# Scale and shift of four feature chunks by multiply-adds on VectorE instead of float32 products on TensorE

## The chip, the cores and the metric

The kernel runs on one core of a Trainium2 chip. The metric is the device time of one execution in microseconds; the figure compared is the median of several runs. The engines of the core are TensorE (PE; its weight loads are PEld), VectorE (DVE), ScalarE (ACT), GpSimd (POOL) and SyncE (SP, which here only issues transfers). Each executes its own instructions in the order in which the program gives them, and waits on semaphores for the others.

## What is computed

Two layers of an encoder trunk on one sequence of 512 rows and 1024 features, all float32. Each of the four sub-layers begins with an adaLN: the rows are normalised, scaled by `norm_g * (1 + scale)` and moved by `shift`; scale and shift come from a vector `c` through a matrix product. The first sub-layer's mixer is a gated convolution.

```python
mod = (jax.nn.silu(c) @ ada_w + ada_b).reshape(bsz, DEPTH, 2, 3, D_MODEL)
for i in range(DEPTH):
    shift, scale, gate = (mod[:, i, 0, k][:, None, :] for k in range(3))
    h = rmsnorm(x, norm_g[i, 0]) * (1.0 + scale) + shift
    if i % N_MIXERS == 0:
        y = short_conv_mixer(h, a_w_in[j], a_conv_w[j], a_w_out[j])
    ...
    x = x + gate * rmsnorm(y, norm_g[i, 1])
    ...
def short_conv_mixer(h, w_in, conv_w, w_out):
    b_gate, c_gate, v = jnp.split(h @ w_in, 3, axis=-1)
    u = causal_depthwise_conv(c_gate * v, conv_w)
    return (b_gate * u) @ w_out
```

## The kernel before

Matrix products take their float32 operands as two parts, a high part (rounded) and a low part (the rest): three matmuls for each product of a weight tile and an activation tile. Features lie on the 128 partitions in eight chunks, 0 to 7; the 512 rows are the free dimension.

The opening, up to about 60 us, does the first adaLN and the first third of the mixer's input product at once. Its order is written out by hand in the string `OPENING`; every name in it is one step, and the engines get their instructions in that order. Of chunk j, `A` multiplies the vector `csil` (silu of c) with the columns of `ada_w` for the chunk's shift and scale on TensorE (16 small float32 matmuls, line 195), `E` copies the sums out (ScalarE, line 199), `T` transposes them (two matmuls, line 202), and `R` adds the bias and makes `mods` (shift) and `acol` (scale) in three small VectorE operations (lines 205 to 208). `u` makes the chunk's scaled value on VectorE (line 360), `H` its high part on ScalarE (line 362), `l` its low part on VectorE (line 364). A step k`j`_`i` is three matmuls of chunk j with one of six weight tiles into accumulator i (line 975, tiles `li`). The weights come in pairs of chunks: a step w`c`l`j` or w`c`b`j` casts the high part of tiles 0 to 3 or of tiles 4 and 5 (ScalarE, line 845), w`s`l`j` and w`s`b`j` make the low part (VectorE, line 847).

The loads are issued by SyncE in program order. `stage_cols` loads the columns of `ada_w` for one or two chunks (tiles `ada_st`, 512 KB each, line 177), `lead_load` the weights of two chunks (`wst_l`, line 830). At most eight transfers of the queue are under way: each issue waits for the one eight before it to land. Chunks 3 and 4 come in one set of four tiles (two for the shift, two for the scale, split along the 1024 inputs), 5 and 6 in another.

Later sets of `ada_w` are not multiplied on TensorE: `ada_madd` (lines 126 and 128) multiplies and adds 1024 columns at a time on VectorE into `ada_acc`, one operation for each of eight blocks of inputs, `ada_fold` (line 141) sums groups of 32 partitions, and a matmul with the 0/1 matrix `four` (line 148) sums the rest.

After the opening the kernel goes on with the mixer's other products (lines 305 to 307), whose weights come in 1 MB loads (line 222).

Of the kernel before, what the change touches and what calls it, by code (L numbers as in the profile page):

```python
# [31 lines left out]
MUL, ADD, SUB = ALU.mult, ALU.add, ALU.subtract  # L32
# [6 lines left out]
def trunk_kernel(  # L39
# [48 lines left out]
    adab = cols2[:, 0:96]  # L88
# [27 lines left out]
    mods = consts.tile([P, 96], F32, name="mods")  # L116
    acol = consts.tile([P, 32], F32, name="acol")
# [6 lines left out]
    def ada_madd(acc, w, k):  # L124
        if k == 0:
            dve.tensor_scalar(acc, w, csil[:, 0:1], None, MUL)
        else:
            dve.scalar_tensor_tensor(acc, w, csil[:, k:k + 1], acc, MUL, ADD)  # L128
# [9 lines left out]
    def ada_fold(acc, dst):  # L138


        dve.tensor_reduce(dst, acc.rearrange("p (b r) -> p b r", r=32), axis=AX.X, op=ADD, apply_transpose=True)
# [20 lines left out]
    def ncol(s, post, j, n=1):  # L162
        i, sub = divmod(s, 2)
        o = (i * 4 + sub * 2 + post) * 8 + j
        return norm_c[:, o:o + n]

    def ada_stage(j0, n, stage):


        res = []  # L170
        for b in range(2):
            c0 = b * D + j0 * P
            parts = []
            for q in range(n):
                st = stage()
                rows = slice(q * D // n, (q + 1) * D // n)
                dma(st, ada_w[rows, c0:c0 + n * P].rearrange("(k p) f -> p k f", p=P))
                parts.append(st)
            res.append(parts)
        return res  # L180
# [150 lines left out]
    def small(n):  # L331
        return tmp.tile([P, n], F32, tag=f"ss{n}", name="ss", bufs=8)
# [19 lines left out]
    def make_h(s, j, hj, src, sl):  # L352

        n = sl.stop - sl.start
        q = s * 24 + j
        us = []

        def value():
            us.append(t2("u")[:, :n])
            dve.tensor_scalar(us[0], src, acol[:, s * 8 + j:s * 8 + j + 1], mods[:, q:q + 1], MUL, ADD)  # L360

        return (value, lambda: act.activation(hj[:, 0, sl], src, AF.Identity, bias=mods[:, q:q + 1],
                                       scale=acol[:, s * 8 + j:s * 8 + j + 1]),
                lambda: dve.tensor_tensor(hj[:, 1, sl], us[0], hj[:, 0, sl].bitcast(F32), SUB))
# [4 lines left out]
    OPENING = """  # L369
xo0 xo1 xo2 xo3 A0b xo4 E0 xo6 xo5 T0 wcl0 R0 u0 q7 H0 wsl0 wcb0 k0a0 l0 xo7 k0a1 k0a2 k0a3 wsb0  # L370
k0c0 k0_4 A1 k0_5 E1 wcl1 T1 k0c1 wcb1 R1 k0c2 k0c3 k0b0 u1 k0b1 H1 k0b2 wsl1 k0b3 l1 A2 wsb1 k1_0
E2 T2 k1_1 R2 wcl2 k1_2 u2 H2 k1_3 wsl2 k1_4 wcb2 l2 k1_5 wsb2 k2_0 k2_1 k2_2 A3 A4 E3 T3 E4 k2_3 R3
T4 u3 H3 k2_4 R4 k2_5 wcl4 l3 u4 H4 k3_0 wsl4 k3_1 wcb4 k3_2 l4 k3_3 wsb4 k3_4 k3_5 k4_0 A5 A6 E5 T5
E6 k4_1 R5 wcl6 T6 u5 k4_2 H5 R6 k4_3 u6 H6 k4_4 l5 wcb6 A7 l6 wsl6 k4_5 E7 T7 wsb6 k5_0 R7 k5_1 u7
k5_2 H7 k5_3 l7 k5_4 k5_5 k6_0 k6_1 k6_2 k6_3 k6_4 k6_5 k7_0 k7_1 k7_2 k7_3 k7_4 k7_5
"""


# [412 lines left out]
    with ExitStack() as ph:  # L791
        sums_p, first_p = ExitStack(), ExitStack()
        gx = ph.enter_context(tc.tile_pool(name="gx", bufs=1, side="right", reuse_waits="tile"))
        ada_p.append(sums_p.enter_context(tc.tile_pool(name="adap", bufs=3, side="right", reuse_waits="tile")))
        actp = first_p.enter_context(tc.tile_pool(name="actp", bufs=22, reuse_waits="tile"))
        four = gx.tile([P, P], F32, tag="four", name="four", bufs=1)
        ada_acc = ada_p[0].tile([P, D], F32, tag="acc", name="ada_acc", bufs=1)
# [71 lines left out]
        staged = []

        def stage_cols(j0, n):
            cols = ada_stage(j0, n, lambda: actp.tile([P, 8 // n, n * P], F32, tag="a", name="ada_st0"))
            staged.extend([(q, cols) for q in range(n)])
# [4 lines left out]
        def turn(t, j):  # L878
            pe.transpose(xtr[j][:, t * P:(t + 1) * P], xn[t][:, j * P:(j + 1) * P], ident)

        def turned_out(j):
            if j % 2 == 0:
                dve.tensor_copy(xf[j], xtr[j])
            else:
                act.copy(xf[j], xtr[j])

        def busy(dst, n):

            for _ in range(n):
                pe.matmul(dst, ident, ident, start=True, stop=True)  # L890
# [11 lines left out]
        with tc.manual_schedule(engines={PE_ENGINE, mybir.EngineType.SP, mybir.EngineType.Activation,  # L902
# [3 lines left out]
                dma(xt[t], x[0, t * P:(t + 1) * P, :])  # L906
            dma_s(rows[:64, 1, :], norm_g.rearrange("i k (r p) -> (i k r) p", p=P))
            dma_s(rows[:96, 2, :], ada_b.rearrange("(r p) -> r p", p=P))
            stage_cols(0, 1)
            load = lead_load(0, 1)  # L910
            next(load)
            next(load)
            stage_cols(1, 1)
            next(load)
            stage_cols(2, 1)
            list(lead_load(1))
            stage_cols(3, 2)
# [60 lines left out]
            def step(name):  # L978
                kind, i = name[:1], name[1:]
                if name[:2] == "xo":  # L980
                    turned_out(int(name[2:]))
                elif name == "q7":
                    xtr.append(aux_ps("xtr"))
                    for t in range(4):
                        turn(t, 7)
                    busy(acc_of(2)[:, :P], 5)
                    h.extend([hp.tile([P, 2, T], F32R, tag=f"h{j}", name=f"h{j}") for j in range(4, KD)])
                elif kind == "A":
                    j = int(i[0])
                    if j:  # L990
                        mods_[j] = ada_first(j, *staged[j], cpad)
                    next(mods_[j])
                    if j == 0:
                        busy(acc_of(2)[:, :P], 2)
                    if j == 4:
                        list(lead_load(3))
                        stage_cols(7, 1)
                elif kind in "ETR":
                    next(mods_[int(i)])
                elif kind in "uHl":  # L1000
                    j = int(i)
                    if j not in hdo:
                        hdo[j] = make_h(0, j, h[j], xf[j], FULL)
                    hdo[j]["uHl".index(kind)]()
                elif kind == "w":
                    kk = int(name[3:])
                    if kk // 2 not in lead:
                        lead_tiles(kk // 2)
                    lead_split(kk // 2, slice(kk % 2, kk % 2 + 1) if kk < 2 else slice(0, 2),
                               "lb".index(name[2]), "cs".index(name[1]))  # L1010
                    if name == "wsb1":
                        list(lead_load(2))
                        stage_cols(5, 2)
# [44 lines left out]
            splits, ws, acts, us, ggs = [], [], [], {}, []  # L1058
# [142 lines left out]
            for k in range(18):  # L1201
                i, jp = k % 6, 2 + k // 6 * 2
# [305 lines left out]
        with tc.manual_schedule(engines={PE_ENGINE, mybir.EngineType.SP, mybir.EngineType.Activation,  # L1508
# [53 lines left out]
            for u in range(UN1):  # L1562
                v = u - 1
# [98 lines left out]
            for k in range(k0, last + 1):  # L1662
# [10 lines left out]
                q, j = divmod(k - 3, 4)  # L1673
# [105 lines left out]
        h, lead_ps, rest, _ = begun  # L1779

    with ExitStack() as ph:
# [301 lines left out]
        four = uh[:, 0:P]  # L2083
# [405 lines left out]
    with ExitStack() as ph:  # L2489
# [137 lines left out]
        with tc.manual_schedule(engines={PE_ENGINE, mybir.EngineType.SP, mybir.EngineType.Activation,  # L2627
# [60 lines left out]
            for u in range(UN):  # L2688
                v = u - 1
# [98 lines left out]
            st = [{"s2": small(2), "s1": small(1), "b1": small(1)} for _ in range(4)]  # L2788
# [133 lines left out]
```

## Time and profile before

| | |
|---|---|
| median of 3 runs | 1308.82 us (1307.88 to 1308.95) |
| span of the profiled execution | 1307.2 us |
| instructions | 20568 |
| moved by transfers | 241.69 MB, mean 185 GB/s |
| 20 to 40 us: transfers | 339 and 348 GB/s |

All times of the prediction are microseconds from the start of the profiled execution's span; its own total lies 1.6 us under the median. A row of a timeline has start, duration, engine, line, operation, the tile written and the tiles read, the shape, and the count of merged instructions; brackets hold the idle time before it and what ended that. A matmul's recorded duration is longer than its share of the engine, since matmuls are pipelined: the distance between starts counts.

### The profile page before, as it was taken

Reading aid. Unit: us, or ns where it says so; the run is one execution under the profiler, and the core shown is the slowest. Engines: PE = TensorE matmul, PEld = TensorE weight load, DVE = VectorE, ACT = ScalarE, POOL = GpSimd, SP = SyncE. Lnnn points to the kernel's source line nnn. Section 1 sums busy time; section 2 is a strip of 40 time slices with the busy share of each in tenths; the row PEclk is TensorE's granted clock in tenths of the full one; section 3 lists DMA queues with packets and bytes.
Section 4 is the critical chain, followed back from the end, with each engine's and each line's share of the span. In section 5 each row is a group of like instructions: output and inputs, shape, how many; then the busy total and the mean of one; then the engine's idle time right before and its main releaser. Section 6 shows DMA issues by size and latency. Waiting matters only on the chain.

```text
span 1307.2 us, 20568 instructions
## 1 busy us (share of the span) xinstructions
PE 1295.7 (99%) x7841; PEld 1140.6 (87%) x7841; DVE 1045.4 (80%) x1598; ACT 736.0 (56%) x1302; POOL 127.5 (10%) x156
## 2 busy tenths in 40 slices
PE   8999999999999999999999999999999999999998
PEld 7788889999988888898888888888899999998886
DVE  5587998978866986769899998987877777767888
ACT  5423466455532565656765567755764555544665
POOL 0000011111100230000000000000100121101320
PEclk9999999999999999999999999999999999999999
DMA  9779661799868984437664456614432788878961
GB/s 310 229 257 297 185 193 50 204 239 240 202 190 264 261 158 119 144 118 231 219 216 160 141 177 217 185 50 161 145 98 72 190 221 204 205 194 286 176 123 64
DMA packets 225942, 241.69 MB, mean 185 GB/s; under 512 B 10532, under 2 KB 177588, under 8 KB 224820
## 3 DMA queue, kind: packets, MB, share of 16 engines
q1 hardware_dynamic: 203200, 192.87, 47.3%
q0 software_dynamic: 18496, 35.92, 15.1%
q10 hardware_dynamic: 4148, 11.59, 2.7%
q8 instruction: 61, 1.00, 0.3%
q14 instruction: 37, 0.30, 0.1%
HBM read 203.76 MB, written 4.34 MB: 159 GB/s over the span
## 4 chain that ended last, share of the span: by engine, by line
PE 94%; DMA 2%; SPq 2%; DVE 1%; ACT 1%; issue 0%; DVEq 0%
PE sA L693 12%; PE ip L305 11%; PE ip L307 11%; PE ip L306 11%; PE y L408 7%; PE sC L693 6%; PE cA L2624 5%; PE sB L693 3%; PE cA L1483 3%; PE li L305 2%; PE li L307 2%; PE li L306 2%; PE li L975 2%; PE y L1156 1%; PE y L2199 1%; PE yd L2027 1%
## 5 line engine op out<-in xcount | busy, mean ns | idle before, releaser
L305 PE MATMUL ip<-h,whl 128*128 128x512 f32 x640 | 253.0, 395 | 0.2 <-DVE cv L1075 0.2
L307 PE MATMUL ip<-h,whl 128*128 128x512 f32 x640 | 249.7, 390 | 0.0
L306 PE MATMUL ip<-h,whl 128*128 128x512 f32 x640 | 249.6, 390 | 0.0
L305 PEld LDWEIGHTS ip<-h,whl 128*128 128x128 f32 x640 | 120.3, 188 | 25.8 <-issue 1.8
L307 PEld LDWEIGHTS ip<-h,whl 128*128 128x128 f32 x640 | 120.3, 188 | 25.3
L306 PEld LDWEIGHTS ip<-h,whl 128*128 128x128 f32 x640 | 120.4, 188 | 23.8
L693 PE MATMUL sA<-tq,whl 128*128 128x256 f32 x1008 | 130.6, 284 | 0.0
L693 PEld LDWEIGHTS sA<-tq,whl 128*128 128x128 f32 x1008 | 125.5, 192 | 0.3
L232 DVE TENSOR_TENSOR whl<-wst,whl 128x1024 fp32r<-128x1024 f32 x70 | 85.2, 1220 | 23.4 <-ACT whl L231 22.3
L128 DVE SCALAR_TENSOR_TENSOR ada_acc<-ada_st,csil,ada_acc 128x1024 f32<-128x1024 f32 x70 | 89.7, 1282 | 3.2 <-DMA ada_st<-in_ada_w_dram 1.9
L305 PE MATMUL li<-h,whl 128*128 128x256 f32 x288 | 83.7, 290 | 0.0
L307 PE MATMUL li<-h,whl 128*128 128x256 f32 x288 | 81.7, 284 | 0.0
L306 PE MATMUL li<-h,whl 128*128 128x256 f32 x288 | 81.6, 283 | 0.0
L231 ACT CAST whl<-wst 128x1024 fp32r<-128x1024 f32 x70 | 72.6, 1040 | 7.8 <-DMA wst<-in_a_w_in_dram 4.0
L408 PE MATMUL y<-whlo,ys 128*128 128x512 f32 x288 | 67.3, 392 | 0.0
L1870 DVE SCALAR_TENSOR_TENSOR cu<-ip,cols,cu 128x511 f32<-128x511 f32 (+2 forms) x84 | 62.8, 747 | 3.4 <-ACT cu L1867 1.4
L408 PEld LDWEIGHTS y<-whlo,ys 128*128 128x128 f32 x288 | 53.8, 188 | 11.4 <-issue 0.5
L2624 PE MATMUL cA<-whlo,ao 128*128 128x512 f32 x264 | 61.0, 391 | 0.4 <-DVE c L2830 0.2
L2624 PEld LDWEIGHTS cA<-whlo,ao 128*128 128x128 f32 x264 | 49.4, 188 | 11.5 <-ACT whlo L2589 1.2
L305 PEld LDWEIGHTS li<-h,whl 128*128 128x128 f32 x288 | 55.3, 192 | 0.8 <-issue 0.8
L306 PEld LDWEIGHTS li<-h,whl 128*128 128x128 f32 x288 | 55.3, 192 | 0.0
L307 PEld LDWEIGHTS li<-h,whl 128*128 128x128 f32 x288 | 55.2, 192 | 0.0
(457 smaller groups left out, 2740.8 us busy)
## 6 DMA issues: line engine op xcount, KB each, us to landing
ada_st<-in_ada_w_dram SPq DMA_DIRECT2D x96, 512.0 KB, 6.4
wsu<-in_f_w_in_dram SPq DMA_DIRECT2D x30, 512.0 KB, 5.5
sg<-in_f_w_in_dram SPq DMA_DIRECT2D x56, 256.0 KB, 3.4
wsu<-in_f_w_in_dram SPq DMA_DIRECT2D x56, 256.0 KB, 4.7
wst<-in_m_w_in_dram SPq DMA_DIRECT2D x14, 1024.0 KB, 5.9
wst<-in_f_w_in_dram SPq DMA_DIRECT2D x10, 1024.0 KB, 5.1
wst<-in_m_w_in_dram SPq DMA_DIRECT2D x20, 512.0 KB, 5.2
wst<-in_a_w_in_dram SPq DMA_DIRECT2D x9, 1024.0 KB, 6.8
```

Of the source, the lines that this page charges most:

```text
L128: dve.scalar_tensor_tensor(acc, w, csil[:, k:k + 1], acc, MUL, ADD)
L231: later.append((lambda sw=sw, w=w: act.copy(w[:, 0, :nk, :], sw), lambda sw=sw, w=w: dve.tensor_tensor(w[:, 1, :nk, :], sw, w[:, 0, :nk, : ...
L232: lambda sw=sw, w=w: dve.tensor_tensor(w[:, 1, :nk, :], sw, w[:, 0, :nk, :].bitcast(F32), SUB)))
L305: pe.matmul(dst, w_at(w, 0, kk), a[:, 0, sl], start=start, stop=False)
L306: pe.matmul(dst, w_at(w, 0, kk), a[:, 1, sl], start=False, stop=False)
L307: pe.matmul(dst, w_at(w, 1, kk), a[:, 0, sl], start=False, stop=stop)
L408: pe.matmul(pst, a[:, al, tk], wt[:, wl, kk, :], start=i == 0 and k == (opens[hf][t] if opens else 0), stop=k == K - 1 and i == 2, skip_gr ...
L693: pe.matmul(dst, w[:, wl, k0 + k, :], self.moving(q, k, al), skip_group_check=True, start=q in self.FIRST and k == 0 and i == 0, stop=k == ...
L975: pe.matmul(acc_of(i), w[:, part // 2, k, c0:c0 + P], h[kk][:, part % 2, :], start=(kk, part) == (0, 0), stop=(kk, part) == (KD - 1, 2))
L1483: pe.matmul(bank[r, sub], a[:, al, q, tk], w[:, wl, q, :], start=first and k == 0, stop=False, skip_group_check=True)
L1870: dve.scalar_tensor_tensor(u[:, sft:], pst[:, :T - sft], w[3 - sft], u[:, sft:], MUL, ADD)
L2624: pe.matmul(bank[r][sub], a[:, al, q, tk], w[:, hl, q, :], start=first and k == 0, stop=last and k == 2, skip_group_check=True)
```

## The change

Shift and scale of chunks 3 and 4, and of 5 and 6, are now made like the later sets. `stage_two` loads, for two chunks, four tiles each with two blocks of inputs, shift and scale side by side: 512 columns in one row, in two loads of 256 KB. Step `M` is one multiply-add of one block (VectorE, 512 columns), `F` the fold, `P` one matmul with `four`, `G` four adds of the bias and one scale. Chunks 0, 1, 2 and 7 stay with TensorE's products. The value `u` of chunks 3 to 7 is made by ScalarE. The order string has new steps and places; `stage_cols(7)` and the weights of chunks 6 and 7 are issued at another step, at the same place of SyncE's order.

```diff
         def value():
             us.append(t2("u")[:, :n])
-            dve.tensor_scalar(us[0], src, acol[:, s * 8 + j:s * 8 + j + 1], mods[:, q:q + 1], MUL, ADD)
+            if j < 3:
+                dve.tensor_scalar(us[0], src, acol[:, s * 8 + j:s * 8 + j + 1], mods[:, q:q + 1], MUL, ADD)
+            else:
+                act.activation(us[0], src, AF.Identity, bias=mods[:, q:q + 1], scale=acol[:, s * 8 + j:s * 8 + j + 1])
...
-E2 T2 k1_1 R2 wcl2 k1_2 u2 H2 k1_3 wsl2 k1_4 wcb2 l2 k1_5 wsb2 k2_0 k2_1 k2_2 A3 A4 E3 T3 E4 k2_3 R3
-T4 u3 H3 k2_4 R4 k2_5 wcl4 l3 u4 H4 k3_0 wsl4 k3_1 wcb4 k3_2 l4 k3_3 wsb4 k3_4 k3_5 k4_0 A5 A6 E5 T5
-E6 k4_1 R5 wcl6 T6 u5 k4_2 H5 R6 k4_3 u6 H6 k4_4 l5 wcb6 A7 l6 wsl6 k4_5 E7 T7 wsb6 k5_0 R7 k5_1 u7
-k5_2 H7 k5_3 l7 k5_4 k5_5 k6_0 k6_1 k6_2 k6_3 k6_4 k6_5 k7_0 k7_1 k7_2 k7_3 k7_4 k7_5
+E2 T2 k1_1 R2 wcl2 k1_2 u2 H2 k1_3 wsl2 k1_4 wcb2 M3_0 l2 k1_5 M3_1 wsb2 M3_2 M3_3 k2_0 M3_4 M3_5 k2_1
+M3_6 M3_7 F3 k2_2 k2_3 P3 G3 u3 H3 k2_4 u4 H4 k2_5 wcl4 l3 wsl4 k3_0 k3_1 l4 wcb4 k3_2 M5_0 M5_1 wsb4
+k3_3 M5_2 M5_3 k3_4 M5_4 M5_5 k3_5 wcl6 k4_0 M5_6 M5_7 F5 k4_1 k4_2 A7 P5 G5 E7 u5 T7 H5 k4_3 R7 u6 H6
+wcb6 k4_4 l5 wsl6 k4_5 l6 u7 H7 wsb6 k5_0 k5_1 k5_2 l7 k5_3 k5_4 k5_5 k6_0 k6_1 k6_2 k6_3 k6_4 k6_5 k7_0
+k7_1 k7_2 k7_3 k7_4 k7_5
...
+        def stage_two(j0):
+
+            two_st[j0] = [actp.tile([P, 2, 2, 2 * P], F32, tag="a", name="ada_st2") for _ in range(KD // 2)]
+            for q, st in enumerate(two_st[j0]):
+                for b in range(2):
+                    dma(st[:, :, b, :], ada_w[2 * q * P:2 * (q + 1) * P, b * D + j0 * P:b * D + (j0 + 2) * P]
+                        .rearrange("(k p) f -> p k f", p=P))
+
+        def two_madd(j0, k):
+            ada_madd(ada_acc[:, 512:], two_st[j0][k // 2][:, k % 2].rearrange("p b f -> p (b f)"), k)
+
+        def two_fold(j0):
+            part = gx.tile([P, 32], F32, tag="fold", name="fold", bufs=2)
+            two_part[j0] = part[:, :16]
+            ada_fold(ada_acc[:, 512:], two_part[j0])
+
+        def two_sum(j0):
+            pt = aux_ps("ada_p2")
+            pe.matmul(pt[:, :16], four, two_part[j0], start=True, stop=True)
+            two_part[j0] = pt
+
+        def two_mods(j0):
+            m2, b2 = [v[:, 0:16].rearrange("p (a b) -> p a b", b=8)[:, :, j0:j0 + 2] for v in (mods, adab)]
+            src = two_part[j0][:, :16].rearrange("p (a q b) -> p a q b", a=2, b=4)
+            for b in range(4):
+                r = slice(b * 32, (b + 1) * 32)
+                dve.tensor_tensor(m2[r], src[r, :, :, b], b2[r], ADD)
+            dve.scalar_tensor_tensor(acol[:, j0:j0 + 2], mods[:, 8 + j0:10 + j0], 1.0, ncol(0, 0, j0, 2), ADD, MUL)
...
+                elif kind == "M":
+                    two_madd(int(i[0]), int(i[2]))
+                elif kind in "FPG":
+                    (two_fold, two_sum, two_mods)["FPG".index(kind)](int(i))
```

TensorE, from the products of chunk 4 (chunk 3's stand just before them) to chunk 3's lead products, before; the tiles `h_124` and `h_125` are chunks 2 and 3:

```order
L195 MATMUL ada_pe<-ada_st_169,rows 32x128 x4
L195 MATMUL ada_pe<-ada_st_171,rows 32x128 x4
L195 MATMUL ada_pe<-ada_st_173,rows 32x128 x4
L195 MATMUL ada_pe<-ada_st_175,rows 32x128 x4
L202 MATMUL ada_pe<-ident,ada_acc 128x128 x2
L975 MATMUL li<-h_124,whl_l 128x512 x3
L202 MATMUL ada_pe<-ident,ada_acc 128x128 x2
L975 MATMUL li<-h_124,whl_b 128x512 x6
L975 MATMUL li<-h_125,whl_l 128x512 x12
```

The same stretch after the change, from chunk 1's last lead products on (line 975 has become 1009):

```order
L1009 MATMUL li<-h_123,whl_b 128x512 x6
L1009 MATMUL li<-h_124,whl_l 128x512 x12
L898 MATMUL ada_p_472<-fold,four 128x16
L1009 MATMUL li<-h_124,whl_b 128x512 x6
L1009 MATMUL li<-h_125,whl_l 128x512 x12
```

The products and both pairs of transposes are gone; one matmul that reads the fold (P3) stands between the fourth and the fifth of chunk 2's six tiles. The second set has the like: P5 stands behind chunk 7's products, with chunk 4's last nine matmuls behind it.

VectorE, before, from the low part of chunk 2's first weights (`whl_l`) to chunk 3's low part:

```order
L847 TENSOR_TENSOR whl_l<-wst_l,whl_l 128x1024
L364 TENSOR_TENSOR h_124<-u,h_124 128x512
L847 TENSOR_TENSOR whl_b<-wst_l,whl_b 128x512
L205 TENSOR_REDUCE ss<-ada_pe 128x2
L207 TENSOR_TENSOR mods<-ss,cols_92 128x2
L208 SCALAR_TENSOR_TENSOR acol<-mods,cols_91 128x1
L360 TENSOR_SCALAR u<-xf,acol,mods 128x512
```

And after, the same stretch:

```order
L851 TENSOR_TENSOR whl_l<-wst_l,whl_l 128x1024
L126 TENSOR_SCALAR ada_acc<-ada_st_169,csil 128x512
L367 TENSOR_TENSOR h_124<-u,h_124 128x512
L128 SCALAR_TENSOR_TENSOR ada_acc<-ada_st_169,csil,ada_acc 128x512
L851 TENSOR_TENSOR whl_b<-wst_l,whl_b 128x512
L128 SCALAR_TENSOR_TENSOR ada_acc<-ada_st_170,csil,ada_acc 128x512 x2
L128 SCALAR_TENSOR_TENSOR ada_acc<-ada_st_171,csil,ada_acc 128x512 x2
L128 SCALAR_TENSOR_TENSOR ada_acc<-ada_st_172,csil,ada_acc 128x512 x2
L141 TENSOR_REDUCE fold<-ada_acc 128x16
L906 TENSOR_TENSOR mods<-ada_p_472,cols_92 32x2x2 x4
L907 SCALAR_TENSOR_TENSOR acol<-mods,cols_91 128x2
L367 TENSOR_TENSOR h_125<-u,h_125 128x512
```

Two multiply-adds have moved in between chunk 2's own operations, and six and the fold stand where VectorE had only small operations; the value `u` is gone from it.

ScalarE, before, from the high part of chunk 2's last weights to chunk 4's (`h3`, `h4` are chunks 3 and 4; the two DMA rows are small loads that ScalarE issues):

```order
L845 CAST whl_b_413<-wst_l_165 128x512
L199 COPY ada_acc_116<-ada_pe_443 128x256
L199 COPY ada_acc_116<-ada_pe_460 128x256
L362 ACTIVATE h3_125<-xf_134,mods_98,acol_99 128x512
L1020 DMA rows_126<-in_a_conv_w_dram 24x128
L1021 DMA dtb_95<-in_m_dt_bias_dram 32x1
L845 CAST whl_l_513<-wst_l_387 128x1024
L362 ACTIVATE h4_305<-xf_135,mods_98,acol_99 128x512
```

And after:

```order
L849 CAST whl_b_421<-wst_l_165 128x512
L363 ACTIVATE u_479<-xf_134,mods_98,acol_99 128x512
L365 ACTIVATE h3_125<-xf_134,mods_98,acol_99 128x512
L363 ACTIVATE u_485<-xf_135,mods_98,acol_99 128x512
L365 ACTIVATE h4_309<-xf_135,mods_98,acol_99 128x512
L1058 DMA rows_126<-in_a_conv_w_dram 24x128
L1059 DMA dtb_95<-in_m_dt_bias_dram 32x1
L849 CAST whl_l_493<-wst_l_391 128x1024
```

The cast of chunk 4's weights (`whl_l`, the last row) now stands behind four scalings and the two small loads.

More of the change, by code (lines that the diff above doesn't have):

```diff
@@ L867, in rows_recip, with stage_cols @@
             dve.reciprocal(ss[:, t:t + 1], ss[:, t:t + 1])
[L869 to L873, printed above, removed]
+        staged = {}
+        def stage_cols(j0):
+            staged[j0] = (0, ada_stage(j0, 1, lambda: actp.tile([P, 8, P], F32, tag="a", name="ada_st0")))
+        two_st, two_part = {}, {}
+        def stage_two(j0):
[21 more added lines that the diff above has]
+            dve.scalar_tensor_tensor(acol[:, j0:j0 + 2], mods[:, 8 + j0:10 + j0], 1.0, ncol(0, 0, j0, 2), ADD, MUL)
         xf = [xf2s[j // 2][:, j % 2, :] for j in range(KD)]
@@ L908, in trunk_kernel @@
             dma_s(rows[:96, 2, :], ada_b.rearrange("(r p) -> r p", p=P))
-            stage_cols(0, 1)
+            stage_cols(0)
             load = lead_load(0, 1)
@@ L912, in trunk_kernel @@
             next(load)
-            stage_cols(1, 1)
+            stage_cols(1)
             next(load)
-            stage_cols(2, 1)
+            stage_cols(2)
             list(lead_load(1))
-            stage_cols(3, 2)
+            stage_two(3)
             turned(rows[:, 0, :], cols1[:, 0:8], 8)
@@ L994, in step @@
                         busy(acc_of(2)[:, :P], 2)
-                    if j == 4:
-                        list(lead_load(3))
-                        stage_cols(7, 1)
+                elif kind == "M":
+                    two_madd(int(i[0]), int(i[2]))
+                elif kind in "FPG":
+                    (two_fold, two_sum, two_mods)["FPG".index(kind)](int(i))
                 elif kind in "ETR":
@@ L1012, in step @@
                         list(lead_load(2))
-                        stage_cols(5, 2)
+                        stage_two(5)
+                    elif name == "wsb2":
+                        list(lead_load(3))
+                        stage_cols(7)
                 elif name[:2] == "k0" and name[2] in "abc":
```

## The prediction

> **What bounds the kernel now.** I read the page's first part, then the busy time of each engine in stretches of the opening, then the chain of waits, and last each engine's order of time between 20 and 53 us, with the landings of the transfers.
>
> ```profile
> PE 1295.7 (99%) x7841; PEld 1140.6 (87%) x7841; DVE 1045.4 (80%) x1598; ACT 736.0 (56%) x1302; POOL 127.5 (10%) x156
> 20.60:27.00 6.40, 6.40 (x59) 4.88 (x58) 4.33 (x12) 4.23 (x8) 0.00 (x0) 1.00 1.11 340
> 27.40:34.00 6.60, 6.37 (x86) 4.93 (x85) 1.80 (x7) 0.83 (x3) 0.00 (x0) 1.00 1.10 349
> ```
>
> In the stretches the columns are length, then PE, PEld, DVE, ACT, POOL busy, the granted clock, the DMA share and GB/s. TensorE is the bound nearly everywhere, so a microsecond that it loses or saves in the opening stays in the total. VectorE works 1.80 of 6.60 us in the second stretch and has room. The DMA engines are full (share above 1, 349 GB/s): in the opening TensorE and the stream of loads both run at their limit.
>
> ```profile
> 28.32 2.20 PE L975 MATMUL li<-h,whl_l 128*128 128x512 f32 x9
> 30.45 0.86 PE L195 MATMUL ada_pe<-ada_st,rows 128*32 128x128 f32 x24
> 31.55 1.30 PE L195 MATMUL ada_pe<-ada_st,rows 128*32 128x128 f32 x40 [0.23 <-DMA ada_st<-in_ada_w_dram]
> 32.78 0.44 PE L202 MATMUL ada_pe<-ident,ada_acc 128*128 128x128 f32 x2
> 32.97 0.94 PE L975 MATMUL li<-h,whl_l 128*128 128x512 f32 x3
> 33.88 1.64 PE L975 MATMUL li<-h,whl_b 128*128 128x512 f32 x6
> 40.44 1.95 PE L195 MATMUL ada_pe<-ada_st,rows 128*32 128x128 f32 x64
> 45.69 1.08 PE L195 MATMUL ada_pe<-ada_st,rows 128*32 128x128 f32 x32
> 47.95 2.99 PE L975 MATMUL li<-h,whl_l 128*128 128x512 f32 x12
> 52.14 1.07 PE L975 MATMUL li<-h,whl_l 128*128 128x512 f32 x4
> 22.79 8.71 DMA ada_st<-in_ada_w_dram
> 27.38 0.71 SPq L177 DMA_DIRECT2D ada_st<-in_ada_w_dram  x1
> ada_st<-in_ada_w_dram SPq DMA_DIRECT2D x1, 512.0 KB, 7.8
> 28.14 1.42 SPq L177 DMA_DIRECT2D ada_st<-in_ada_w_dram  x1
> ada_st<-in_ada_w_dram SPq DMA_DIRECT2D x1, 512.0 KB, 8.6
> 36.72 0.37 SPq L177 DMA_DIRECT2D ada_st<-in_ada_w_dram  x1
> ada_st<-in_ada_w_dram SPq DMA_DIRECT2D x1, 512.0 KB, 7.1
> ```
>
> The first rows are TensorE's order of time (start, duration). A chunk's lead products are 18 matmuls: chunk 5's start at 47.95, chunk 6's at 52.14, so 0.23 us each. The row at 22.79 is the chain's: the last of the four tiles for chunks 3 and 4 lands at 31.50, and TensorE waits for it. Each row with KB belongs to the transfer issued in the row above it and ends in the time to landing: the tiles for chunks 5 and 6 land at 35.2 and 36.7, one per 1.5 us, so the next two at about 38.2 and 39.7; chunk 7's first lands at 43.8, its second then at about 45.3.
>
> **What the change removes from TensorE.** The products of chunks 3 and 4 occupy 30.45 to 32.78 (2.3 us with their wait), those of 5 and 6 1.9, and four pairs of transposes 0.19 each (32.78 to 32.97), 0.8 together. Two small matmuls come back at about 0.3 each by the next section's L148 row. If nothing else ended later, TensorE would save about 4.4 us.
>
> **What it adds on VectorE.** Per pair of chunks: one multiply, seven multiply-adds of 512 elements, one fold, four adds and one scale.
>
> ```profile
> 26.20 1.22 DVE L847 TENSOR_TENSOR whl_l<-wst_l,whl_l 128x1024 fp32r<-128x1024 f32 x1
> 27.34 0.69 DVE L364 TENSOR_TENSOR h<-u,h 128x512 fp32r<-128x512 f32 x1
> 27.94 0.69 DVE L847 TENSOR_TENSOR whl_b<-wst_l,whl_b 128x512 fp32r<-128x512 f32 x1
> 63.97 1.53 DVE L1084 SCALAR_TENSOR_TENSOR u_cv<-cv,cols,u_cv 128x511 f32<-128x511 f32 x2
> 102.42 2.60 DVE L128 SCALAR_TENSOR_TENSOR ada_acc<-ada_st,csil,ada_acc 128x1024 f32<-128x1024 f32 x2
> L141 DVE TRANSPOSE_TENSOR_REDUCE fold<-ada_acc x3: 1234/1239/1242, 92.2 to 161.1; 128x32 f32<-128x1024 f32 x3
> 11.42 0.48 DVE L861 TENSOR_SCALAR xn<-x,ss 128x512 f32<-128x512 f32 x1
> 110.43 0.68 DVE L152 TENSOR_TENSOR mods<-ada_ps,cols 32x8 f32<-32x8 f32 x4
> L128 DVE SCALAR_TENSOR_TENSOR ada_acc<-ada_st,csil,ada_acc x27: 1276/1280/1287, 70.4 to 294.0; 128x1024 f32<-128x1024 f32 x27
> 104.28 0.30 PE L148 MATMUL ada_ps<-fold,four 128*128 128x32 f32 x2
> ```
>
> No multiply-add of 512 elements on this accumulator is in the trace. Nearest are the two chained taps of L1084 (511 elements): 0.75 long, the second starting 0.78 after the first. The 1024-element pair agrees: 2.60 for two of 1.28 leaves a start every 1.32, so a chained one waits for the one before it. I take **0.78**. Bounds: 0.60, the step between independent 512-element operations (27.34 to 27.94), and 0.83 with one more semaphore. The first multiply is 0.48, and 0.40 when its successor doesn't need it. The fold is 1.24 at 1024 elements; a half lies between 0.62 and 1.24, and I take 0.70, half with a start-up. The four adds take 0.68, the scale 0.16.
>
> **First wait (matmul P3, behind k2_3).** VectorE keeps its order up to the low part of chunk 2's weights at 26.20. Then: multiply M3_0 27.34, l2 27.74 (0.4 later than before), M3_1 28.34, weights wsb2 29.0, and from 29.6 six chained multiply-adds at 0.78 to 34.3. The data is there: tile 4 (31.50) is needed only at 32.7. The fold ends at 35.0. TensorE has k2_0 to k2_3 meanwhile, 12 matmuls from 28.3, done at 31.2. P3 stands next in its queue, in front of k2_4 and k2_5 which could run, so **TensorE idles about 3.7 us**. P3 ends at 35.4; adds and scale at 36.3.
>
> ```profile
> 33.91 0.82 ACT L362 ACTIVATE h<-xf,mods,acol 128x512 fp32r<-128x512 f32 x1 [0.57 <-DVE acol L208]
> 35.65 1.05 ACT L845 CAST whl_l<-wst_l 128x1024 fp32r<-128x1024 f32 x1 [0.92 <-DMA ada_st<-in_ada_w_dram]
> 43.73 1.60 ACT L362 ACTIVATE h<-xf,mods,acol 128x512 fp32r<-128x512 f32 x2
> 49.15 0.82 ACT L362 ACTIVATE h<-xf,mods,acol 128x512 fp32r<-128x512 f32 x1 [1.89 <-DVE acol L208]
> 50.00 0.69 DVE L364 TENSOR_TENSOR h<-u,h 128x512 fp32r<-128x512 f32 x1 [0.30 <-ACT h L362]
> ```
>
> The new scaling on ScalarE has no row; it is H's operation (0.82 alone, 0.8 each in a pair, a start every 0.72) with another output. So u3 36.36, H3 37.08, and l3 on VectorE 0.85 behind H's start, as at 49.15 and 50.00: 37.9 to 38.6. Chunk 3's second matmul needs l3; the last 17 of its 18 take until 42.6.
>
> **Second wait (P5, behind chunk 7's products).** ScalarE does u4 and H4 before the weights of chunk 4: 37.8, 38.5 to 39.3. Two small loads stand in its queue behind H4, each waiting for a lane whose last transfer (tiles 3 and 4 of chunks 5 and 6) lands at 38.2 and 39.0; the row at 35.65 shows that such a wait holds ScalarE. They clear just in time; each microsecond later costs one. The cast runs 39.35 to 40.4, and VectorE, idle since 38.6, does wsl4 40.4, l4 41.6, M5_0 42.2, M5_1 42.7, wsb4 43.35, six multiply-adds from 43.95, and the fold 48.6 to 49.3. TensorE does k4_0 to k4_2 (9 matmuls to 44.7) and chunk 7's products, to 45.9 by the landing at 45.3, then **idles 3.5 us** until P5 at 49.4. Adds and scale end at 50.7, u5 and H5 to 52.2, l5 to 53.0; the transposes, k4_3 to k4_5 and the small ones are through by 52.1 and hide behind that. Chunk 5's second matmul starts at 53.0, and 17 matmuls later chunk 6 begins at **56.9 against 52.14: +4.8 us**.
>
> **What hides.** Five values move from VectorE to ScalarE (0.72 each). For chunks 6 and 7 they lie under k5 to k7, some 13 us; without that cover they cost 0.72 each. The sixteen half-size loads in place of eight carry the same bytes, and eight may be in flight, 2 MB, or 6 us at 349 GB/s, so I expect the same landings; the first wait has 1.2 us to spare on them, the second 2.5. The next two 1 MB loads go out later, behind wsb4 and wsb6: the second only at 55.6.
>
> ```profile
> wst<-in_a_w_in_dram SPq DMA_DIRECT2D x1, 1024.0 KB, 5.1
> 64.78 1.04 ACT L231 CAST whl<-wst 128x1024 fp32r<-128x1024 f32 x1
> ```
>
> With 5.1 to landing it is there at 60.7; its first reader, at 64.78 now, moves to 69.6: nine microseconds of cover. Behind the opening each engine's order is unchanged, so the shift stays: span 1307.2 + 4.8 = 1312.0, and the median, 1.6 above the profiled span, 1308.82 + 4.8 = **1313.6**. Its own bounds: multiply-adds at 0.60 take off 2.2 (six steps in each of two chains, 0.18 each), a fold of 1.24 adds 1.1, ScalarE at 0.82 in place of 0.72 another 0.6: 1311.4 to 1315.3.
>
> **Rivals.**
>
> *VectorE keeps up (not slower).* Were a chained multiply-add cheaper, both waits shrink together. Six steps in each chain count, so from 0.60 down the loss falls under 2.6 us (0.2%, about what a measurement can tell from no change). For: both chains are on one engine that is idle half the time, and wsl4's wait for ScalarE might be shorter. Against: both pairs of rows, and the landings. Tile 4 at 31.5 and chunk 7's second at 45.3 allow no chunk 6 before about 52.7, since P5, the transposes and nine matmuls now stand behind chunk 7's products, where three stood. Time 1309.3 to 1311.4, chance 0.13.
>
> *The saving comes through (faster).* If neither small matmul waited, 1308.8 - 4.4 = 1304.4. It takes both folds done by 31.2 and 45.9; the first would precede its own data's landing at 31.50. Chance 0.03.
>
> *The clock falls in a gap.*
>
> ```profile
> 1295.68 5.22 PE L2624 MATMUL cA<-whlo,ao 128*128 128x512 f32 x22
> 1304.00:1306.00 2.00, 0.00 (x0) 0.00 (x0) 0.20 (x1) 0.00 (x0) 0.00 (x0) 0.86 0.71 235
> 1306.00:1308.00 2.00, 0.00 (x0) 0.00 (x0) 0.00 (x0) 0.00 (x0) 0.00 (x0) 0.50 0.00 0
> ```
>
> The last matmul ends at 1300.9; a mean of 0.86 between 1.00 and 0.50 puts the fall at 1305.4, after 4.5 us without work. The new gaps are 3.7 and 3.5. Halved behind the first, chunks 3 and 4 would eat the idle time in front of P5 and cost little. Halved behind the second, k4_3 to k4_5 end 1.4 past 53.0, and chunk 5 may take up to 4 more: about 3 on top, 1316.6. Chance 0.06.
> The Trainium skill, "TensorE: Matmul & The Clock Gate", section "Part 1: The HAM clock gate (the "warmup" mystery)", has the clock halve after one whole idle window of about 3.4 us, with windows that run freely. By that rule a gap of 3.7 us seldom holds a whole window; the fall after 4.5 us agrees with it. By it the sum stays at 1313.6; by a gate that falls sooner it is 1316.6.
>
> **How the numbers follow.** The forecast has 0.78, VectorE keeping up 0.13, the clock 0.06, the saving 0.03. Slower by over 0.2% is 0.84, within 0.2% 0.13, faster 0.03. The range runs from 1310.5, under the forecast's own low end, to 1317.0, over the clock's 1316.6.
>
> **What would show it.** TensorE idle for about 3.7 and 3.5 us in front of the matmuls on fold, each ended by VectorE's fold; a start every 0.78 us in the chains; VectorE idle for about 1.8 us until ScalarE's cast of chunk 4's weights; chunk 6's first matmul at 56.9; from there the same distances as before. A chain step near 0.6, a landing after 32.7, or later stages that move by another amount would make it wrong.

## The result and the profile after

The changed kernel is slower, by more than forecast.

| | before | after |
|---|---|---|
| median | 1308.88 us of 4 runs (1307.88 to 1311.00) | 1320.18 us of 4 runs (1318.71 to 1322.01) |
| ratio, 95% interval | | 1.0085 (1.0073 to 1.0097) |
| profiled execution: span | 1307.2 us | 1320.2 us |
| chunk 6's first matmul | 52.14 | 59.80 |

A second set of 5 runs of the same kernel (e12_again, below) gave 1319.87 us and a ratio of 1.0090 (1.0076 to 1.0104). The forecast was 1313.6, its range 1310.5 to 1317.0: the direction was right, the size about 2.4 times too small (11.3 us for 4.8).

First the opening, in TensorE's order of time after the change (start, duration, idle time before in brackets), with one row from much later at the end:

```profile
35.55 0.39 PE L898 MATMUL ada_p<-fold,four 128*128 128x16 f32 x2 [3.92 <-DVE fold L141]
35.78 2.91 PE L1009 MATMUL li<-h,whl_b 128*128 128x512 f32 x6
...
49.91 0.58 PE L898 MATMUL ada_p<-fold,four 128*128 128x16 f32 x2 [3.52 <-DVE fold L141]
...
52.08 2.76 PE L1009 MATMUL li<-h,whl_b 128*128 128x512 f32 x6
...
55.00 3.61 PE L1009 MATMUL li<-h,whl_l 128*128 128x512 f32 x12
58.45 1.52 PE L1009 MATMUL li<-h,whl_b 128*128 128x512 f32 x6
59.80 2.43 PE L1009 MATMUL li<-h,whl_l 128*128 128x512 f32 x10
...
264.41 1.85 PE L697 MATMUL sA<-tq,whl 128*128 128x256 f32 x7 [1.85 <-ACT g L707]
```

The two gaps are where they were forecast, 3.92 and 3.52 long, and VectorE's fold ends each. What wasn't forecast stands behind them: six matmuls take 2.91 and 2.76 where the same six take 1.52 at 58.45. And there is a third gap at 262.56 to 264.41, far behind the opening. VectorE's rows of the same stretch:

```profile
29.98 4.68 DVE L128 SCALAR_TENSOR_TENSOR ada_acc<-ada_st,csil,ada_acc 128x512 f32<-128x512 f32 x6
34.70 0.71 DVE L141 TRANSPOSE_TENSOR_REDUCE fold<-ada_acc 128x16 f32<-128x512 f32 x1
...
40.81 1.23 DVE L851 TENSOR_TENSOR whl_l<-wst_l,whl_l 128x1024 fp32r<-128x1024 f32 x1 [1.66 <-ACT whl_l L849]
```

Six chained multiply-adds take 4.68, that is 0.78 each, the fold 0.71, and VectorE's wait for ScalarE's cast is 1.66 (forecast 0.78, 0.70 and about 1.8). The busy time in stretches of 3.41 us shows why the matmuls behind the gaps are slow (columns as in the prediction: length, PE, PEld, DVE, ACT, POOL busy, granted clock, DMA share, GB/s):

```profile
32.35:35.76 3.41, 0.20 (x2) 0.24 (x3) 2.95 (x4) 0.00 (x0) 0.00 (x0) 1.00 1.10 349
35.76:39.18 3.42, 3.42 (x9) 2.11 (x8) 1.50 (x6) 2.28 (x4) 0.00 (x0) 0.50 1.11 349
46.00:49.42 3.42, 0.40 (x16) 0.13 (x7) 3.28 (x5) 0.37 (x1) 0.00 (x0) 1.00 0.84 288
49.42:52.83 3.41, 2.92 (x9) 2.56 (x10) 1.63 (x9) 1.39 (x2) 0.00 (x0) 0.50 0.00 0
52.83:56.24 3.41, 3.41 (x9) 2.23 (x9) 2.96 (x5) 3.41 (x6) 0.00 (x0) 0.50 0.00 0
261.05:264.46 3.41, 1.55 (x14) 1.35 (x12) 3.31 (x7) 2.54 (x5) 0.00 (x0) 1.00 0.91 221
264.46:267.87 3.41, 3.41 (x16) 3.41 (x17) 3.41 (x6) 1.12 (x2) 1.69 (x2) 0.50 0.88 249
```

The granted clock is 0.50 from 35.76 to 39.18, from 49.42 to 56.24 and from 264.46 to 267.87. Its changes lie on one grid of 3.413 us: the second and third fall stand 4 and 67 such steps behind the first. Each fall stands at the end of a grid window in which TensorE was busy for 0.20, 0.40 or 1.55 us. None of them was wholly idle.

The third gap begins on ScalarE. Its order of time after the change, then before:

```profile
245.08 1.06 ACT L752 ACTIVATE tq<-va 128x1024 fp32r<-128x1024 f32 x1 [8.04 <-PE li L307]
```

```profile
230.91 1.06 ACT L748 ACTIVATE tq<-va 128x1024 fp32r<-128x1024 f32 x1 [1.58 <-DVE va L759]
```

The operation moves by 14.17 us while everything round it has moved by 7.7, and it waits for TensorE where it waited for VectorE. The order of instructions is the same in both kernels. What differs is memory. The staging tiles and, later, the lead weights of the feed-forward take turns in the 22 buffers of one rotating pool. `tq1`, the tile written here, belongs to a later pool that is laid over the same memory. By the addresses in the two programs it covers four of these buffers, and it can be written only when their last readers are done. Before the change, chunk 7's two staging buffers were used again after all four of chunks 5 and 6; now they come ahead of three of those four, which VectorE reads up to its last multiply-adds. From there on the buffers are handed out in another order. Before, none of the four under `tq1` held a lead weight last; now one does, and TensorE reads it until late in the lead products.

Adding up the profiled execution: +7.7 in the opening, +2.2 at the third gap, +1.8 from the half clock behind it, +1.7 between 446 and 460, -0.3 near 570: 13.1 for a span 13.0 longer. This execution, 1322.01 us, is the slowest of the four; between the medians lie 11.3.

### The profile page after: what moved, and what is told of

Its sections match the earlier page's. It is cut to its first block, busy times and chain, and to the rows that moved or that the text cites. A ratio compares the mean times of both kernels' runs of the same rounds, so it can differ in the third digit from the quotient of the medians.

```text
span 1320.2 us, 20325 instructions
## 1 busy us (share of the span) xinstructions
PE 1297.5 (98%) x7709; PEld 1140.7 (86%) x7709; DVE 1055.2 (80%) x1609; ACT 738.4 (56%) x1303; POOL 127.9 (10%) x156
## 4 chain that ended last, share of the span: by engine, by line
PE 93%; DVE 2%; DMA 2%; SPq 1%; ACT 1%; issue 1%; DVEq 0%; ACTq 0%
PE sA L697 12%; PE ip L305 11%; PE ip L307 11%; PE ip L306 11%; PE y L412 7%; PE sC L697 6%; PE cA L2662 4%; PE cA L1521 3%; PE sB L697 3%; PE li L305 3%; PE li L307 3%; PE li L306 3%; DMA ada_st<-in_ada_w_dram 1%; PE y L1194 1%; PE y L2237 1%; PE yd L2065 1%
## 5 line engine op out<-in xcount | busy, mean ns | idle before, releaser
L128 DVE SCALAR_TENSOR_TENSOR ada_acc<-ada_st,csil,ada_acc 128x1024 f32<-128x1024 f32 (+1 forms) x84 | 100.3, 1194 | 3.3 <-DMA ada_st<-in_ada_w_dram 1.7
```

## Experiments

Chunk 6's first matmul marks the end of the opening; in the trace of before it is at 52.14. "Shift" is how much later an instruction starts than in that trace.

### Fillers in the gaps

```diff
-            pt = aux_ps("ada_p2")
+            pt = aux_ps("ada_p2"); busy(pt[:, P:2 * P], {3: 12, 5: 10}[j0])
```

> The changed kernel, with small matmuls on the identity matrix in TensorE's two gaps (12 of them, about 3.0 us, ahead of P3, and 10, about 2.5 us, ahead of P5); they write columns that nobody reads. Theory (half of the surplus over the forecast is TensorE's clock, halved behind each gap): no half clock between 30 and 60 us; k4_3 to chunk 5 at full speed, so that chunk 6's first matmul moves from 59.80 back to 57.2 to 57.6, with P3 and P5 where they were (35.5, 49.9). The later wait of ScalarE's tq<-va stays, so the span falls by 2.2 to 2.6, from 1320.2 to about 1317.8; if the gap at 262.6 then lies otherwise in the clock's windows of 3.41 us, its halving may go too, another 1.8. Rival (the clock only accompanies it, chunk 5 is late by VectorE and ScalarE): chunk 6 stays within 0.4 of 59.8 and the time at 1320.

1318.14 us (1317.49 to 1318.89), ratio 1.0070 (1.0057 to 1.0083); span 1317.1. TensorE in the profile:

```profile
53.70 2.79 PE L1009 MATMUL li<-h,whl_l 128*128 128x512 f32 x11 [0.23 <-DVE h L367]
56.33 1.52 PE L1009 MATMUL li<-h,whl_b 128*128 128x512 f32 x6
57.69 2.88 PE L1009 MATMUL li<-h,whl_l 128*128 128x512 f32 x12
```

No half clock in the opening, and chunk 6 at 57.69, 0.1 above the theory's range and 2.1 ahead of after, with P3 and P5 within 0.3 of after's (35.82, 50.06). With the clock whole, chunk 5's second matmul waits for VectorE's low part, as the forecast had it. The wait of `tq<-va` stayed, with a gap of 1.85 at 260.44. The windows of e1_fill there:

```profile
257.64:261.05 3.41, 2.80 (x24) 2.59 (x22) 2.63 (x5) 1.87 (x4) 0.00 (x0) 1.00 1.05 208
261.05:264.46 3.41, 2.17 (x18) 2.17 (x19) 3.41 (x6) 2.41 (x4) 1.10 (x2) 1.00 0.91 256
```

A gap as long as the third one of after falls across two windows here, and the clock stays whole. A second gap of 1.42 follows at 266.86, and the shift still grows by 3.9 there, from 5.6 to 9.5; the median fell by 2.0.

### Another order of the buffers

The pool gives out buffers in the order of the tiles' first writes, so the order of eight weight splits decides which tile lies where. (A split is the step that makes a weight tile's high and low part.)

```diff
-            for op in todo[3] + todo[4] + todo[1] + todo[2]:
+            for op in todo[3] + todo[4] + todo[1][:1] + todo[1][2:] + todo[2][:2] + todo[1][1:2] + todo[2][2:]:
```

> The changed kernel, with the split of one lead weight tile of the feed-forward (the second half of its third column block) moved four casts later, so that the buffer in which tq1 is written later holds this tile, which TensorE is done with 54 matmuls (6.5 us) sooner, in place of the one that it reads last but one. Nothing in the opening is touched. Theory (the change handed the buffers out in another order, and a write of ScalarE waits for TensorE to be done with a weight): tq<-va starts at about 238.6 in place of 245.08, TensorE's gap at 262.6 goes (1.86 us) and the half clock behind it (1.8 us); the shift against before stays at +7.7 up to 400 us, and the span is 1316.5 if the later 1.3 us stay, 1315.2 if they go with it. Rival (ScalarE is late there because the opening is late): tq<-va stays at 245 and the time at 1320.

1318.35 us (1314.67 to 1319.39), ratio 1.0067 (1.0055 to 1.0080); span 1316.6. ScalarE's order of time in e2_slots:

```profile
237.45 1.06 ACT L752 ACTIVATE tq<-va 128x1024 fp32r<-128x1024 f32 x1 [1.65 <-DVE va L763]
```

It waits for VectorE again and is shifted by 6.5, as the opening is (chunk 6 at 58.57, +6.43), and the gap at 262 is gone. But another took its place, 1.42 at 265.59, and VectorE's order of time shows from where:

```profile
252.27 0.69 DVE L676 TENSOR_TENSOR sg<-sg,wsu 128x512 f32<-128x512 f32 x1 [1.71 <-DMA sg<-sg]
```

The new order had put a weight tile that is read longer into the buffer of `sg`, whose load was issued at 240.24 in place of about 237.3 (230.88 before, plus the shift). The span is the theory's upper value, 1316.5, but not for its reasons: the opening was 1.2 shorter this time (the clock was halved for 3.41 us behind the second gap, not 6.83), and the late `sg` load cost 1.75. Both edits together:

> Both edits, the fillers in the two gaps and the moved split. Theory (two separate causes, the clock in the opening and the buffer): the savings add up, shift about +5.3 behind the opening and from there on, span 1312.5 to 1313.8, median 1314.1 to 1315.4. Rival (one cause, of which the other is a consequence): no better than the better one of the two alone.

1316.46 us (1316.25 to 1317.28), ratio 1.0059 (1.0045 to 1.0073); span 1314.4. The savings add up: 3.7 of the 11.3, where the two edits alone gave 2.0 and 1.8. The opening's shift is 5.43, but the median is 1.1 above the range given. The late `sg` load is in this kernel too, and the shift grows by 2.6 between 250 and 270. So a third order was tried that leaves neither `tq1` nor `sg` with a late tile.

```diff
-            for op in todo[3] + todo[4] + todo[1] + todo[2]:
+            for op in todo[3] + todo[4] + [todo[1][2], todo[1][0], todo[1][3], *todo[2][:2], todo[1][1], *todo[2][2:]]:
```

> The changed kernel with the feed-forward's lead weight tiles split in another order, chosen so that tq1's buffer gets a tile that TensorE is done with 54 matmuls sooner, as in e2_slots, and sg's buffer one that it is done with no later than before (in e2_slots sg's load of the next weights was issued 2.9 us later than in the kernel before, measured against the shift). Theory (only the late reader of a buffer costs): tq<-va on ScalarE follows VectorE's va as in e2_slots; no gap over 0.8 us of TensorE between 240 and 270; shift against before stays near that of the opening, +6.4 to +7.7; span 1315 to 1316.5 by whether the 1.3 us after 440 appear. Rival (ScalarE and VectorE are late there by the shift itself): gaps of 1.4 to 1.9 us remain and the time is that of e2_slots, 1318.3.

1316.13 us (1313.40 to 1316.70), ratio 1.0049 (1.0037 to 1.0062); span 1314.7. No gap over 0.8 between 240 and 270; the shift is 5.2 to 5.4 from the opening to 440, under the 6.4 to 7.7 named, since the clock fell behind the first gap alone. Near 446 +1.8 appear, more than the 1.3 named, and +0.4 near 560.

> The fillers of e1_fill and the order of e6_slots2. Theory (the forecast's +4.8 was right for the opening, and the rest was the clock and the buffers): shift +5.4 behind the opening and +5 to +5.6 at the end, span 1312.2 to 1312.9, median 1313.7 to 1314.6. Rival (something else behind the opening costs as well): over 1315.5.

1314.16 us (1314.04 to 1314.53), ratio 1.0040 (1.0026 to 1.0054); span 1312.4. This is the changed kernel without the half clock and without the late tiles, and it stands 0.6 from the forecast's 1313.6. A part of that is luck: its opening ends at +5.9 (chunk 6 at 58.06), above the +5.4 expected, and behind 440 the shift falls to +5.2, which is not explained. In its profile `tq<-va` and TensorE run through:

```profile
236.95 1.06 ACT L752 ACTIVATE tq<-va 128x1024 fp32r<-128x1024 f32 x1 [1.65 <-DVE va L763]
```

```profile
257.64 1.60 PE L697 MATMUL sC<-tq,whl 128*128 128x256 f32 x12
259.08 1.60 PE L697 MATMUL sB<-h,whl 128*128 128x256 f32 x12
260.52 1.60 PE L697 MATMUL sA<-tq,whl 128*128 128x256 f32 x12
```

### Fillers in the second gap alone

`{3: 12, 5: 10}` of e1_fill becomes `{3: 0, 5: 10}`.

> The changed kernel with the 10 fillers ahead of P5 only; the first gap is left empty. Theory (the forecast's step on the clock: a halving behind the first gap is eaten by the wait ahead of P5): half clock from about 36 us for 3.4 us, none behind P5, and chunk 6's first matmul as in e1_fill, 57.6 within 0.3; whether the time behind differs from e1_fill is for the buffers. Rival (the first halving delays chunk 4 and with it VectorE's second chain): chunk 6 at 58.2 or later.

Span 1317.2, one run of 1319.01 us. The clock was halved from 33.79 to 40.62, twice as long as expected, and chunk 6 still came at 57.57: the theory's number. In this profile the halving behind the first gap cost nothing. Behind the opening a gap of 1.85 (260.32 to 262.18) lay in one window this time, as the busy time by windows of e8_fill5 shows, and the clock fell:

```profile
259.08:262.49 3.41, 1.56 (x13) 1.36 (x12) 3.31 (x6) 2.80 (x6) 0.33 (x1) 1.00 0.78 206
262.49:265.90 3.41, 3.41 (x18) 3.41 (x17) 3.41 (x5) 0.85 (x1) 1.39 (x2) 0.50 1.16 294
```

### The same kernel again

> The changed kernel once more, nothing edited, for a second profile of the same instructions. Theory (what the clock costs depends on where its windows of 3.41 us lie against the two gaps): P3 and P5 stand as before (35.5, 49.9 or, with a long halving behind the first gap, the same), each gap's windows that are mostly idle are followed by half clock, and chunk 6's first matmul lies anywhere from 57.4 to 59.8 by their phase; tq<-va waits as in the first profile, for TensorE, about 6.5 us beyond the shift. Rival (the clock's cost is fixed by the program): chunk 6 at 59.8 within 0.3 again. Whether the long issue of the wst load (1.64 us at 413) comes again is open to both.

1319.87 us (1318.53 to 1323.33); span 1318.1. TensorE's order of time in this second profile, then three of its windows:

```profile
35.19 1.93 PE L1009 MATMUL li<-h,whl_b 128*128 128x512 f32 x6
...
49.39 0.37 PE L898 MATMUL ada_p<-fold,four 128*128 128x16 f32 x2 [1.45 <-DVE fold L141]
...
57.01 2.88 PE L1009 MATMUL li<-h,whl_l 128*128 128x512 f32 x12
```

```profile
32.93:36.35 3.42, 1.38 (x7) 1.23 (x8) 2.63 (x8) 0.06 (x1) 0.00 (x0) 1.00 1.10 347
36.35:39.76 3.41, 2.66 (x7) 1.31 (x6) 0.69 (x1) 3.41 (x5) 0.00 (x0) 0.50 1.10 348
...
258.22:261.64 3.42, 1.56 (x14) 1.35 (x13) 3.32 (x7) 2.51 (x5) 0.00 (x0) 1.00 0.80 183
```

Not one instruction differs from after, and chunk 6 is at 57.01 for 59.80, 0.4 ahead of the range expected: +4.87, where the forecast said +4.8. About 0.6 of the 2.8 is an earlier start (P3 at 34.97 for 35.55), the rest is the clock. The windows lie otherwise against P3's gap: one begins 1.87 behind the gap's start (31.06) in place of 0.71 (31.64). The halving behind it lasted two windows, so that chunks 3 and 4 ran on into the second gap, which shrank to 1.45, and the clock held behind it. A long halving at the harmless place prevented the harmful one. Yet the median of the five runs is where it was: most of the loss lies behind the opening. There `tq<-va` waits 8.04 for TensorE again (242.29), the gap at 259.76 is 1.86 without a halving, the 1.42 gap follows at 266.20, and the shift is 8.75. In the first profile the half clock stood in place of the 1.42 gap; either way the buffer costs 3.9 to 4.0. The gap of 1.86 lies in one window with 1.56 us of work (the last row above), as the like gap does in after and in e8_fill5, where the clock fell. So how a gap lies in its windows doesn't settle it alone.

### One pair of chunks, and ScalarE's part alone

> The kernel before, with the value u of chunks 3 to 7 made by ScalarE and nothing else of the change. Theory (the move to ScalarE hides under TensorE's products, as forecast): chunk 6's first matmul within 0.5 of 52.14, median 1308.3 to 1310. Rival (u and H one after the other on ScalarE, 0.72 a chunk, delay chunks 3 to 5 by themselves): up to 2.2 us slower, 1311.

The edit is the first hunk of the change's diff, made in the kernel before. 1309.50 us of 11 runs (1308.84 to 1310.17) against 1308.94, ratio 1.0005 (0.9996 to 1.0013): no difference that can be measured. Chunk 6 moved by 0.91 in the profile, a little more than the 0.5 allowed; at the end of it 0.5 are left.

> Only chunks 5 and 6 by VectorE's multiply-adds; 3 and 4 by TensorE's products as before (and u of chunks 3 to 7 by ScalarE). Its multiply-adds are placed in between from wsl4 on. Worked out from the rows of before and after: wsl4 ends at about 38, eight multiply-adds with l4 and wsb4 in between and the fold to 46.0, P5 at 46.3 behind chunk 7's products (second landing 45.3), scale 47.2, u5 and H5 to 48.7, l5 49.4, chunk 6 17 matmuls later. Theory (the loss comes of two chains, the first of which holds the second up): chunk 6's first matmul at 53 to 54, so +1 to +2 for this pair alone. Rival (the second chain alone costs it all): +4 or more, 56 to 57.

Span 1311.4, one run of 1313.17 us; chunk 6 at 56.47, so the expectation failed by 2.5, and the rival's 56 to 57 came. ScalarE's order of time in e9_pair5 shows what it had left out:

```profile
36.79 0.32 ACTq L1059 DMA_DIRECT2D rows<-in_a_conv_w_dram  x1
38.32 0.33 ACTq L1060 DMA_DIRECT2D dtb<-in_m_dt_bias_dram  x1
38.69 1.05 ACT L849 CAST whl_l<-wst_l 128x1024 fp32r<-128x1024 f32 x1 [3.50 <-DMA ada_st<-in_ada_w_dram]
```

Two small loads stand ahead of the cast of chunk 4's weights and hold it until transfers land that were issued eight before them. The clock fell here too, from 43.47 to 46.89, behind a window with 1.19 us of work. The loads were moved:

```diff
+                    if name == "wcl6":
+                        dma_s(rows[:24, 3, :], a_conv_w.rearrange("i k (r p) -> (i k r) p", p=P))
+                        dma_s(dtb[:NH], m_dt_bias.rearrange("i (r p) -> (i r) p", p=1))
...
-                    if (kk, i) == (2, 5):
+                    if False:
                         dma_s(rows[:24, 3, :], a_conv_w.rearrange("i k (r p) -> (i k r) p", p=P))
                         dma_s(dtb[:NH], m_dt_bias.rearrange("i (r p) -> (i r) p", p=1))
```

> The kernel of e9_pair5 with one thing moved: the two small loads that ScalarE issues go out behind the cast of chunk 6's weights instead of ahead of the cast of chunk 4's. In e9_pair5 they held ScalarE for 3.50 us (before: 0.92), since each waits for the transfer eight issues back and the 5-and-6 set now takes eight issues in place of four. Theory (that wait made e9_pair5 miss its 53 to 54): wcl4 starts at about 35.2 in place of 38.69, the fold ends at about 45.5 in place of 48.6, chunk 6's first matmul at 53 to 54, a shift of +1 to +2 behind the opening, median 1310 to 1311. Rival (VectorE's chain alone makes it late): chunk 6 stays at 56 to 57.

1311.78 us of 10 runs (1310.40 to 1315.04), ratio 1.0024 (1.0014 to 1.0034); span 1309.2. Rows of ScalarE, VectorE and TensorE in e10_loads:

```profile
35.15 1.03 ACT L849 CAST whl_l<-wst_l 128x1024 fp32r<-128x1024 f32 x1
...
44.33 0.71 DVE L141 TRANSPOSE_TENSOR_REDUCE fold<-ada_acc 128x16 f32<-128x512 f32 x1
...
53.70 0.62 PE L1010 MATMUL li<-h,whl_l 128*128 128x512 f32 x2
```

The cast starts at 35.15, the fold ends at 45.04 and chunk 6 begins at 53.70, +1.56, as expected, and the clock stays whole. The profiled run, 1311.06 us, lies in the range given to 0.1; the median is 0.8 over it, which one profile doesn't explain. So the second pair alone costs about 1.6 in the opening, in this placement. By difference the first pair, whose chain pushes the second's back, costs the rest of the 4.9 to 5.5; it was not run alone.

> The kernel of e10_loads with P5 and k4_5 ahead of chunk 7's products (which wait for their load) and seven small matmuls on the identity ahead of P5 to keep the clock: the best place for one pair on VectorE that I see. Worked out as before: fold 45.4, P5 45.6, scale 46.4, u5 and H5 to 48.0, l5 48.8, chunk 6 at 52.5 to 53, so +0.4 to +0.9 against before, median 1309 to 1310: level with the kernel before within what can be measured. Rival (the products taken from TensorE come through): chunk 6 at 51 or earlier, median 1307.5 or less.

```diff
-M5_5 k3_5 M5_6 M5_7 F5 k4_0 k4_1 wcl6 k4_2 k4_3 k4_4 A7 P5 G5 E7 u5 T7 H5 k4_5 R7 u6 H6
+M5_5 k3_5 M5_6 M5_7 F5 k4_0 k4_1 wcl6 k4_2 k4_3 k4_4 P5 G5 k4_5 A7 u5 E7 T7 H5 R7 u6 H6
...
-            pt = aux_ps("ada_p2")
+            pt = aux_ps("ada_p2"); busy(pt[:, P:2 * P], {3: 0, 5: 7}[j0])
```

1312.33 us of 10 runs (1310.69 to 1313.78), ratio 1.0024 (1.0015 to 1.0034); span 1311.4. Neither expectation held: chunk 6 came at 56.13, 3 us later than worked out. P5 was at 45.53 as worked out, but the copy of chunk 7's sums stood ahead of H5 on ScalarE, so that H5 began at 48.62, where it was to end at 48.0, and a window that was idle for 1.38 of its 3.41 us was followed by half clock in the middle of chunk 5. The windows of e11_best:

```profile
48.21:51.62 3.41, 2.03 (x8) 1.29 (x9) 2.23 (x6) 3.27 (x6) 0.00 (x0) 1.00 0.01 2
51.62:55.03 3.41, 3.41 (x10) 2.64 (x9) 1.88 (x3) 1.15 (x2) 0.00 (x0) 0.50 0.22 65
```

None of the kernels tried beats the kernel before; e4_scal is level with it.

## Why the prediction was right in the opening and wrong in sum

- **The chains and the two gaps: right.** 0.78 a step, fold 0.71, gaps 3.92 and 3.52 (forecast 3.7 and 3.5), about 0.5 later than forecast (P3 35.55 for 35.0, P5 49.91 for 49.4), mostly since the first chain began at 29.98 for 29.6. The second profile ends the opening at +4.87, e6_slots2 at +5.2; with fillers it is +5.4 to +5.9. The forecast's 4.8 was the size, at the low end.
- **What hides: right.** ScalarE's share costs nothing that can be told from no change (e4_scal), and VectorE waited 1.66 for the cast of chunk 4's weights, where about 1.8 was forecast.
- **"The clock falls in a gap", chance 0.06: wrong in the chance.** It fell behind one gap or both in all four profiles of this opening without fillers (after, e2_slots, e6_slots2, e12_again). The price was about right where it counts (up to 2.4 by e6_slots2 against after, 57.35 for 59.80), and that a halving behind the first gap is absorbed was right (e8_fill5). The step that failed held that a gap of 3.7 us would seldom bring a fall; it had one row with a fall, after 4.5 us without work. The windows before the falls of after had 0.20, 0.40 and 1.55 us of work, so a window need not be wholly idle. The Trainium skill ("TensorE: Matmul & The Clock Gate", section "Part 1: The HAM clock gate (the "warmup" mystery)") gives at least one idle window of about 3.4 us as the condition. The prediction read that as a wholly idle window, and read so it doesn't agree with these windows. The same section says that the window runs free of the kernel and that effects vary from run to run; with that the two profiles of one kernel agree, 59.80 and 57.01.
- **"Behind the opening each engine's order is unchanged, so the shift stays": the step that failed most.** The order did stay; the buffers did not. The step put nothing for them, and the third gap and what follows it cost 3.9 to 4.0. In e6_slots2 and e7_both2 the shift stays within 0.2 from the opening to 440, once the tiles lie elsewhere. The forecast looked at who stands where in a queue, and not at which buffer a tile gets when others are released in another order.
- **Between 446 and 460: open.** There after loses 1.7 more and e12_again 2.4. SyncE's rows before, and after:

```profile
401.72 0.54 SPq L1659 DMA_DIRECT2D wst<-in_f_w_in_dram  x1
```

```profile
413.36 1.64 SPq L1697 DMA_DIRECT2D wst<-in_f_w_in_dram  x1
```

This issue takes 1.41 to 1.69 in the four profiles of the opening without fillers and 0.43 to 0.56 in all others, and its load lands 6.6 to 7.4 us after it in place of 5.0 to 5.6. The traces show one thing more. In each of the four, a 16 KB transfer of the kind "instruction" begins 0.12 to 0.19 us after the issue and takes 0.92 to 1.20; in no other profile does one begin during this issue. Such transfers come once for about every 256 of TensorE's matmuls and weight loads, so that more or fewer matmuls in the opening move them. Whether they lengthen the issue was not tried. Nor is it all: up to 0.8 appear at this place in e1_fill, e8_fill5 and e10_loads without the long issue.

## What to carry to other kernels

That an engine's order is unchanged doesn't mean that its waits are: where a change lets go of buffers of a rotating pool in another order, look at which buffer each later tile gets, and at who still reads what lay there. A stall of TensorE has two prices, its own length and the clock behind it; the second depends on where the windows lie, so profile the same kernel twice before a microsecond or two is explained, and fill gaps with work that nobody reads: one gap of 1.85 us was enough for a fall in two of the profiles. Count transfers as well as bytes: in e9_pair5, with one set's loads cut in half, a wait for the eighth one back was 3.50 us long where it had been 0.92.

## What the runs showed that was not expected

In all profiles the clock changes on a grid of 3.413 us, which lies otherwise against the kernel from run to run. By the share of a window between 20 and 1300 us in which no matmul is recorded: at 59.7% idle or more the clock was halved in all 8 cases; under 40% in none; between 40 and 55% in 3 of 13. At 54.3% it was halved in after and e8_fill5 and not in e6_slots2, so the share of idle time alone doesn't decide there; what else does is open. Once halved, it came back after windows of 10.4% idle and less, and stayed for another window at 14.6% and more (4 cases), so a short gap behind a halving lengthens it to 6.83 us. With fillers the runs also spread less: 0.5 us in e7_both2, against 3.3 in e6_slots2 with the same buffers and no fillers, five runs each.
